# A hybrid diffusion backbone on one core: the RWKV-7 units without GpSimd instructions

## The chip, the core and the metric

The program runs on one core of one Trainium2 chip. The metric is the device time of one execution in microseconds (us); lower is better. The engines are named as in the profile: PE (matrix products, with its weight loads as PEld), DVE (vector), ACT (scalar), POOL (GpSimd) and SP, whose queue issues the DMAs spoken of here.

## What is computed

Layer 0 is attention and is not touched. Layer 1 runs two branches on 1024 latent and 256 context tokens, and the change is in its RWKV-7 branch: 8 heads of 64 features, scanned in both directions, first over the context and then over the latents.

```python
kk = k * k_k;  kk = kk * rsqrt(sum(kk * kk, per head) + 1e-12)
for d in (forward, backward):
    decay = exp(-exp(w_log[d]))                  # w_log: a gate of every token and feature
    a = sigmoid(a0[d] + da @ a_up[d])
    k_d = k * (1 + (a - 1) * k_a);   b = kk * a
    s = s * decay - (s @ kk) b^T + v k_d^T       # per token, s is 64 x 64
    y = s @ r
out = groupnorm(y_fwd + y_bwd) + sum(r * (k_fwd + k_bwd)/2 * r_k) * v
x = x + gate * ([out * silu(g), hyena] @ w_out);   rms_norm(x)
```

## The kernel before, in words

All products that need accuracy are made from float32 values split in two parts, "hi" and "lo": `split` copies the hi part on ACT (L164) and subtracts it for the lo part (L168) on POOL, or on DVE where `lo_eng="v"`.

**Projections** (`gemm3`, to about 1796 us). Blocks of 128 columns of the input projection follow each other: values, keys (`rw_keys`, four blocks, one for each pair of heads j), then four blocks of r. Each block is 48 or 72 products g_ps at L363 out of `mm3`, and needs its weights split on DVE (w_lo, L168). `rw_gates` runs beside them: the decay gates so go token by token to the DRAM tensor SG (L1266), the rates a to AS (L1275). `rw_keys` makes kk with a reciprocal on DVE (L1219) and stores kk and k in KK (L1223). An r block ends with one DVE instruction rwo (L1028) and a store to US.

**Units** (`rwkv`). There are 8 jobs (j, d) of 5 units, 40 units in all, each of 256 tokens (4 chunks of 64) for two heads. The loop over units b issues `rw_solve` for b+2, `rw_front` for b+12, `rw_trans` and `rw_scan` for b; a list scheduler then sets the final order on each engine from its own estimates, and each engine works through its list in order.

- `rw_front` loads kk and k (kkf, L1381), a (af), the gates (sg, L1386) and v, splits the gates (ACT, then POOL), forms running sums cs_ps on PE (L1397), then exponentials on ACT (E and AKR). POOL makes `kd` in two steps (L1417, L1419), `af` (L1420) and half of BK (L1426); DVE the other half (L1424) and AK, AR (L1415, L1414). PE forms the Gram matrices g_ps (L1442), four products for head 0 and then four for head 1, with 64 rows each. DVE masks one half of g_ps to la (L1443); the other half goes through an ACT copy (L1446) and a POOL mask (L1447) into gm. ACT copies the off-diagonal blocks of la into LO (L1452), a tile whose other entries are zero. la's diagonal blocks go by DMA to lanes (LD, L1458).
- `rw_invert` inverts these blocks of 32 tokens for a job at once: L1495 and L1497 on DVE, 31 steps of two instructions each, from L (loaded from LD) to XD. The first job does it in two parts (units 0 to 1, then 2 to 4), the others in one.
- `rw_solve` (L1522) is y = XT R, z = LO Z, R = R - z on DVE (L1529), w = XT R: three groups of four products of 128 rows and 128 columns, all in one PSUM bank "s".
- `rw_trans` makes the transitions ph_ps (L1555). `rw_scan` carries the state over the four chunks: st_ps (L1579, L1582), one ACT copy S (L1583), and two ACT copies into a block-diagonal tile (L1590) for the output product L1591; L1593 adds gm times UV after each chunk.
- `rw_bonus` and `rw_readout` serve the 16 backward latent units; five POOL instructions on [128, 4] (L1640 to L1647) are the group norm's root, L1614 to L1617 the bonus, L1656 the gate.

Every float32 product stands twice in the profile, as two MATMUL records; the scheduler's listing below has it once. So g_ps with 8 products a unit has 16 records.

**Final** (`Final`, from unit 28 on) prepares the output projection in the room that the units leave: `weights` loads rec_w_out in 16 pieces, multiplies by the gate (POOL, L1943) and splits it; `project` makes fe_ps (L363).

The PSUM tiles of a front take turns in two banks "f"; "s" and "p" hold one tile at a time:

```python
FB = 2
PB = (1, 1, 1, 1, 1)                          # banks s, p, t, y, r
tags = [...  for t in ("sfff" if self.nfront < 5 else "rfty" if self.nfront < 10 else "ffff")]
ps = self.rps([128, 4, 128], "g_ps", *tags[1])          # in rw_front, once for each head
ps = self.rps([128, 2, 512], "ph_ps", "p", PB[1])       # in rw_trans
```

## Time and profile before

| | |
|---|---|
| median of 3 runs | 2480.67 us (2476.8 to 2485.05) |
| profiled execution, first to last instruction | 2478.4 us |
| PE busy | 2300.1 us (93%), 16639 products |
| DVE busy | 1543.9 us (62%), 3275 instructions |
| ACT busy | 1191.4 us (48%), 2815 instructions |
| POOL busy | 981.2 us (40%), 1071 instructions |
| DMA | 357.09 MB, 144 GB/s on average |

The profiled execution has no time of its own beside its span; the span lies 2.3 us under the median of the runs. The page's slices and the table of stretches tell which engine is full where; the groups by line tell what one instruction of a kind takes and which wait ended before it; the timeline tells what ran beside what.

### The profile page before, as it was taken

Reading aid. Unit: us, or ns where it says so; the run is one execution under the profiler, and the core shown is the slowest. Engines: PE = TensorE matmul, PEld = TensorE weight load, DVE = VectorE, ACT = ScalarE, POOL = GpSimd, SP = SyncE. Lnnn points to the kernel's source line nnn. Section 1 sums busy time; section 2 is a strip of 40 time slices with the busy share of each in tenths; the row PEclk is TensorE's granted clock in tenths of the full one; section 3 lists DMA queues with packets and bytes.
Section 4 is the critical chain, followed back from the end, with each engine's and each line's share of the span. In section 5 each row is a group of like instructions: output and inputs, shape, how many; then the busy total and the mean of one; then the engine's idle time right before and its main releaser. Section 6 shows DMA issues by size and latency. Waiting matters only on the chain. (4 is left out here: it accounts for less than half of the span.)

```text
span 2478.4 us, 45316 instructions
## 1 busy us (share of the span) xinstructions
PE 2300.1 (93%) x16639; PEld 1883.1 (76%) x16639; DVE 1543.9 (62%) x3275; ACT 1191.4 (48%) x2815; POOL 981.2 (40%) x1071
## 2 busy tenths in 40 slices
PE   5999999999999998888899999899977999999997
...
GB/s 280 129 128 115 127 157 145 221 165 38 112 82 77 158 174 188 177 185 178 156 133 135 124 225 138 147 215 184 158 111 111 121 113 131 114 130 132 170 81 95
DMA packets 337269, 357.09 MB, mean 144 GB/s; under 512 B 80082, under 2 KB 274911, under 8 KB 336278
## 3 DMA queue, kind: packets, MB, share of 16 engines
...
q0 software_dynamic: 144, 4.19, 0.4%
...
## 5 line engine op out<-in xcount | busy, mean ns | idle before, releaser
L363 PE MATMUL g_ps<-xl,w_hi 128*128 128x512 f32 x1056 | 269.3, 401 | 1.0 <-ACT w_hi L164 1.0
L363 PEld LDWEIGHTS g_ps<-xl,w_hi 128*128 128x128 f32 x1056 | 200.2, 192 | 44.3 <-issue 1.9
L413 POOL TENSOR_TENSOR al_acc<-al_acc,al_t 128x512 f32<-128x512 f32 x98 | 130.0, 1327 | 182.7 <-ACT al_t L411 153.0
L168 DVE TENSOR_TENSOR w_lo<-w_raw,w_hi 128x256 fp32r<-128x256 f32 (+1 forms) x184 | 126.8, 745 | 78.6 <-PE g_ps L363 40.3
L159 ACT COPY pt<-pt_ps 128x512 f32<-128x512 f32 (+1 forms) x235 | 105.9, 459 | 138.1 <-PE pt_ps L641 136.3
L630 PE MATMUL s_ps<-k,q 128*128 128x256 f32 (+1 forms) x352 | 140.3, 405 | 18.6 <-DMA k<-ka 11.2
L1497 DVE TENSOR_TENSOR X<-X,tmp 80x112 f32<-80x112 f32 (+25 forms) x279 | 139.0, 498 | 6.7 <-DVE tmp L1495 0.2
L1495 DVE TENSOR_TENSOR tmp<-L,X 80x112 f32<-80x112 f32 (+25 forms) x279 | 130.5, 468 | 13.2 <-DMA L<-LD 7.0
L363 PE MATMUL g_ps<-xl,w_lo 128*128 128x512 f32 x528 | 138.3, 396 | 0.0
L363 PE MATMUL g_ps<-xhi,w_hi 128*128 128x512 f32 (+1 forms) x528 | 119.0, 368 | 9.3 <-DVE ac_res L255 4.7
L631 PE MATMUL s_ps<-k,q 128*128 128x256 f32 (+1 forms) x352 | 118.0, 341 | 4.9 <-DMA k<-ka 4.9
L411 ACT ACTIVATE al_t<-al_w,condT 128x512 f32<-128x512 f32 x98 | 70.8, 722 | 102.8 <-POOL al_acc L413 63.7
L658 ACT ACTIVATE p<-p,mn 128x1280 f32<-128x1280 f32 (+1 forms) x96 | 103.4, 1077 | 31.9 <-DVE p L655 30.1
L363 PE MATMUL g_ps<-xhi,w_lo 128*128 128x512 f32 (+1 forms) x528 | 118.3, 363 | 0.0
L363 PEld LDWEIGHTS g_ps<-xl,w_lo 128*128 128x128 f32 x528 | 98.6, 189 | 21.2 <-issue 1.4
L363 PEld LDWEIGHTS g_ps<-xhi,w_hi 128*128 128x128 f32 x528 | 90.4, 194 | 31.0 <-DVE qraw L521 6.1
L363 PE MATMUL g_ps<-xlo,w_hi 128*128 128x512 f32 (+1 forms) x528 | 112.8, 356 | 0.0
L641 PE MATMUL pt_ps<-ident,p 128*128 128x128 f32 x704 | 110.8, 280 | 1.5 <-ACT pt L159 0.6
L168 POOL TENSOR_TENSOR hz<-hfull,hz 128x256 fp32r<-128x256 f32 x64 | 47.4, 742 | 152.9 <-ACT hz L164 152.2
L669 PE MATMUL o_ps<-pt,vb 128*64 128x128 f32 x1344 | 104.6, 279 | 0.0
L363 PEld LDWEIGHTS g_ps<-xhi,w_lo 128*128 128x128 f32 x528 | 89.6, 191 | 18.1 <-issue 5.0
L800 POOL TENSOR_TENSOR bias<-namask,tt 128x384 f32<-128x384 f32 x64 | 64.8, 1021 | 97.3 <-DMA tt<-TG 39.6
...
## 6 DMA issues: line engine op xcount, KB each, us to landing
...
```

The source lines that it names most:

```text
L159: self.nc.scalar.copy(out=out, in_=in_)
L168: e.tensor_tensor(out=lo, in0=full, in1=hi.bitcast(F32), op=ALU.subtract)
L363: nc.tensor.matmul(ps, x(k), y(k), start=(n == 0), stop=(n == 3 * nk - 1))
L411: nc.scalar.activation(out=o, in_=wt, func=AF.Copy, scale=self.condT[:, k, ci:ci + 1])
L413: nc.gpsimd.tensor_tensor(out=t, in0=t, in1=o, op=ALU.add)
L630: self.nc.tensor.matmul(ps, q, k[0][ks], start=True, stop=False)
L631: self.nc.tensor.matmul(ps, q, k[1][ks], start=False, stop=True)
L641: nc.tensor.transpose(ps[:, c, :], p[:, (c4 + c) * 128:(c4 + c + 1) * 128], self.ident)
L658: nc.scalar.activation(out=p[:, 0:nk], in_=p[:, 0:nk], func=AF.Exp, bias=mn, scale=-1.0, accum_out=rs[:, hh:hh + 1])
L669: nc.tensor.matmul(o[64 * hh:64 * hh + 64, :], v[c][hh], pts[hh][:, c, :], start=(c == 0), stop=(c == nch - 1), tile_position=(0, 64 * hh))
L1495: nc.vector.tensor_tensor(out=tv, in0=L[:, s:s + 1, rt].to_broadcast([n, nj, nt]), in1=X[:, rj, s:s + 1].to_broadcast([n, nj, nt]), op=ALU ...
L1497: nc.vector.tensor_tensor(out=X[:, rj, rt], in0=X[:, rj, rt], in1=tv, op=ALU.subtract)
```

## The change

All that POOL did for the units moves or goes. (1) `rw_keys` forms b = kk a and k_d for both directions beside the projections and stores kk, b and k_d in KB (one for each direction); `rw_gates` splits the gates there and stores both parts. A front then loads both ready. (2) Both masks are applied on DVE straight from PSUM, into one tile LG that holds gm (columns 0 to 63) and la (64 to 127). (3) The Gram products alternate between the heads, in two banks. (4) LO is gone: the solve multiplies 32 x 32 blocks of LG, and the correction is added to w_ps in PSUM by a second product instead of a subtraction on DVE. (5) The state is written by two ACT copies straight into the block-diagonal tile, and the four products of gm with UV stand together ahead of the chunks. (6) Bonus, readout and the final weights use DVE.

The diff, cut to its core:

```diff
@@ rw_keys
-        for i, t in enumerate((kk, o)):
-            nc.sync.dma_start(out=self.KK[rows, :, i, :], in_=t.rearrange("p (q t) -> p q t", t=256))
+        for d in range(2):
+            b = sp.tile([128, NT], F32, name="kb", tag="lraw", bufs=2)
+            nc.sync.dma_start(out=b, in_=self.AS[d][rows, :])
+            kd = sp.tile([128, NT], F32, name="kd", tag="kd", bufs=1)
+            nc.scalar.activation(out=kd, in_=b, func=AF.Identity, scale=self.col("rwkv_k_a", j), bias=self.oka[:, j:j + 1])
+            nc.vector.tensor_tensor(out=kd, in0=kd, in1=o, op=ALU.mult)
+            nc.vector.tensor_tensor(out=b, in0=b, in1=kk, op=ALU.mult)
+            for i, t in enumerate((kk, b, kd)):
+                nc.sync.dma_start(out=self.KB[d][rows, :, i, :], in_=t.rearrange("p (q t) -> p q t", t=256))
@@ rw_gates
-                nc.sync.dma_start(out=self.SG[d][tt * 128:tt * 128 + 128, :], in_=so)
+                sh = sp.tile([128, 2, 512], F32R, name="sh", tag="sh", bufs=2)
+                self.split(sh[:, 0], sh[:, 1], so, lo_eng="v")
+                for part in range(2):
+                    nc.sync.dma_start(out=self.SG[d][tt // 2, :, :, part, tt % 2, :], ...)
@@ rw_front
-... ("sfff" if self.nfront < 5 else "rfty" if self.nfront < 10 else "ffff")]
+... ("sffff" if self.nfront < 5 else "rffty" if self.nfront < 10 else "fffff")]
-        self.split(sgs[:, 0], sgs[:, 1], sg)
-            nc.vector.tensor_tensor(out=AR, in0=AR, in1=v3(rf), op=ALU.mult)
-        nc.vector.tensor_tensor(out=AK, in0=AK, in1=kv, op=ALU.mult)
-        nc.gpsimd.tensor_scalar(out=kd, in0=v3(af), scalar1=self.col("rwkv_k_a", j), ...)
-        nc.gpsimd.tensor_tensor(out=kd, in0=kd, in1=kf, op=ALU.mult)
-        nc.gpsimd.tensor_tensor(out=v3(af), in0=v3(af), in1=kv, op=ALU.mult)
+            nc.vector.tensor_tensor(out=AKR, in0=AKR, in1=kb[:, 0:2].rearrange(...), op=ALU.mult)
-        self.last_bk = nc.gpsimd.tensor_tensor(out=BK[:, :, 64:192], in0=kd, in1=E, op=ALU.mult)
+        nc.vector.tensor_tensor(out=BK[:, :, 64:192], in0=v3(kb[:, 3]), in1=E, op=ALU.mult)
+        gp = [self.rps([128, 4, 128], "g_ps", *tags[1 + h]) for h in range(2)]
+        for ci in range(4):
+            for h in range(2):
+                z = slice(64 * h, 64 * h + 64)
+                nc.tensor.matmul(gp[h][:, ci, c0:128], BK[z, i, 128 * c:128 * c + 128], ...)
         for h in range(2):
-            nc.vector.tensor_tensor(out=la[:, h], in0=ps[:, :, 0:64], in1=mask[:, 0:64]..., op=ALU.mult)
-                nc.scalar.copy(out=gm[:, h], in_=ps[:, :, 64:128])
-                nc.gpsimd.tensor_tensor(out=gm[:, h], in0=gm[:, h], in1=mask[:, 64:128]..., op=ALU.mult)
-            for c in range(2):
-                nc.scalar.copy(out=LO[zs, 2 * h:2 * h + 2, t1:t1 + 32], in_=la[zs, h, c::2, t0:t0 + 32])
+            nc.vector.tensor_tensor(out=LG[:, h, :, c0:128], in0=gp[h][:, :, c0:128], in1=mask[:, c0:128]..., op=ALU.mult)
@@ rw_solve
-        ps = prod(xt, R, "y_ps")
+        ps = self.rps([128, 4, 128], "w_ps", "s", PB[0])
+        for u in range(4):
+            nc.tensor.matmul(ps[:, u, :], xt[:, u, :], R[:, u, :], start=(u == 0), stop=True, skip_group_check=True)
         nc.scalar.copy(out=Z, in_=ps)
-        ps = prod(LO, Z, "z_ps")
-        nc.vector.tensor_tensor(out=R, in0=R, in1=ps, op=ALU.subtract)
-        ps = prod(xt, R, "w_ps")
+        pz = self.rps([128, 2, 512], "z_ps", "p", PB[1])...
+        for u in range(4):
+            for c in range(2):
+                nc.tensor.matmul(pz[zt, u, :], LG[zs, h, 2 * i + c, 64 + t0:96 + t0], Z[zs, u, :], ...,
+                                 tile_position=(64 * c + s0, 64 * c + t0))
+        for c in range(2):
+            nc.scalar.activation(out=Z[zt], in_=pz[zt], func=AF.Copy, scale=-1.0)
+        for u in range(4):
+            for c in range(2):
+                nc.tensor.matmul(ps[zt, u, :], xt[zt, u, zt], Z[zt, u, :], start=False, stop=True, ...,
+                                 tile_position=(64 * c + t0, 64 * c + t0))
@@ rw_scan
+        if lat:
+            for i in range(2):
+                for h, zo in heads:
+                    for c in range(2):
+                        nc.tensor.matmul(yp[64 * c:64 * c + 64, i, zo], LG[:, h, 2 * i + c, 0:64], UV[:, i, c, h, :],
+                                         start=(i == 0 and h == 0), stop=False, tile_position=(0, 64 * c))
-            nc.scalar.activation(out=n, in_=ps, func=AF.Copy, scale=Dt[:, n0 + ci:n0 + ci + 1])
+            for h, zo in heads:
+                nc.scalar.activation(out=n[zo, zo], in_=ps[zo], func=AF.Copy, scale=Dt[zo, n0 + ci:n0 + ci + 1])
-                    nc.scalar.copy(out=sd[zo, zo], in_=S[zo])
-                    nc.tensor.matmul(yp[zc, i, zo], gm[:, h, ci, :], UV[:, i, c, h, :], ...)
@@ rw_bonus, rw_readout, Final.weights
-        nc.gpsimd.tensor_tensor(out=a0, in0=a0, in1=a1, op=ALU.add)
+        nc.vector.tensor_tensor(out=a0, in0=a0, in1=a1, op=ALU.add)
-        e = nc.gpsimd
+        e = nc.vector
-        nc.gpsimd.tensor_tensor(out=t, in0=t, in1=g, op=ALU.mult)
+        nc.vector.tensor_tensor(out=t, in0=t, in1=g, op=ALU.mult)
-            self.nc.gpsimd.tensor_tensor(out=raw, in0=raw, in1=self.gate1[h], op=ALU.mult)
-            self.k.split(tiles[0][h], tiles[1][h], raw)
+            self.nc.vector.tensor_tensor(out=raw, in0=raw, in1=self.gate1[h], op=ALU.mult)
+            self.k.split(tiles[0][h], tiles[1][h], raw, lo_eng="v")
```

The scheduler's listing shows where this moves work. On PE, at the end of the projections, before the change (g_ps<-xl is the projection, cs_ps the first step of a front, g_ps<-AKR its Gram products):

```order
L363 MATMUL g_ps<-xl_12457,w_lo 128x512 x8
L363 MATMUL g_ps<-xl_12457,w_hi 128x512 x3
L1397 MATMUL cs_ps<-tri,sgs 128x256
L363 MATMUL g_ps<-xl_12457,w_hi 128x512 x5
L363 MATMUL g_ps<-xl_12458,w_hi 128x512
L1397 MATMUL cs_ps<-tri,sgs 128x256 x3
L363 MATMUL g_ps<-xl_12458,w_hi 128x512 x7
L363 MATMUL g_ps<-xl_12457,w_lo 128x512 x8
L363 MATMUL g_ps<-xl_12457,w_hi 128x512 x8
L1397 MATMUL cs_ps<-tri,sgs 128x256 x4
L363 MATMUL g_ps<-xl_12458,w_hi 128x512 x4
L1442 MATMUL g_ps<-AKR,BK 128x64 x8
```

And now:

```order
L363 MATMUL g_ps<-xl_12458,w_hi 128x512 x8
L363 MATMUL g_ps<-xl_12459,w_hi 128x512 x8
L363 MATMUL g_ps<-xl_12458,w_lo 128x512 x8
L1402 MATMUL cs_ps<-tri,sgs 128x256 x8
L1436 MATMUL g_ps<-AKR,BK 128x64 x8
L1402 MATMUL cs_ps<-tri,sgs 128x256 x4
L1450 MATMUL bk_ps<-ident,BK 128x128 x4
L1457 MATMUL rh_ps<-ident,AKR 128x2x64 x2
```

The first steps of the fronts stood among the last two blocks of the projection; they now follow its last product.

On PE in the middle of the units, before (y_ps and z_ps are the solve, yo_ps<-UV,gm the second output product):

```order
L1522 MATMUL y_ps<-R,XT_18018 128x128 x4
L1579 MATMUL st_ps<-UV,BT 64x64 x2
L1582 MATMUL st_ps<-S,PH 64x64 x2
L1397 MATMUL cs_ps<-tri,sgs 128x256
L1591 MATMUL yo_ps<-S_18035,RT 64x128
L1593 MATMUL yo_ps<-UV,gm 64x64 x2
L1397 MATMUL cs_ps<-tri,sgs 128x256 x3
L1555 MATMUL ph_ps<-BT,At 64x64 x2
L1522 MATMUL z_ps<-Z,LO_17313 128x128 x4
L1579 MATMUL st_ps<-UV,BT 64x64 x2
L1582 MATMUL st_ps<-S,PH 64x64 x2
```

And now:

```order
L1577 MATMUL yo_ps<-UV,LG 64x64 x8
L1586 MATMUL st_ps<-UV,BT 64x64 x2
L1589 MATMUL st_ps<-S_18070,PH 64x64 x2
L1595 MATMUL yo_ps<-S_18070,RT 64x128
L1402 MATMUL cs_ps<-tri,sgs 128x256 x3
L1520 MATMUL z_ps<-Z,LG 32x128 x8
L1586 MATMUL st_ps<-UV,BT 64x64 x2
L1589 MATMUL st_ps<-S_18071,PH 64x64 x2
L1595 MATMUL yo_ps<-S_18071,RT 64x128
L1648 MATMUL yt_ps<-ident,Y 128x128 x2
L1528 MATMUL w_ps<-Z,XT_18060 32x128 x8
L1554 MATMUL ph_ps<-BT,At 64x64 x8
```

The output products stand in one group of eight, and the solve's second and third group have eight products of 32 x 128 in place of four of 128 x 128.

On DVE, at the last key block, before (RECIPROCAL is L1219, w_lo the weights of the next projection block, LO the zeroed tiles):

```order
L1219 RECIPROCAL ksq<-ksq 128x256
L168 TENSOR_TENSOR w_lo<-w_raw,w_hi 128x256 x4
L1219 RECIPROCAL ksq<-ksq 128x512
L1028 SCALAR_TENSOR_TENSOR rwo<-rws,hm,rwo 128x1024
L1219 RECIPROCAL ksq<-ksq 128x512
L168 TENSOR_TENSOR w_lo<-w_raw,w_hi 128x256 x4
L1169 MEMSET LO_17312 128x512
```

And now:

```order
L1216 RECIPROCAL ksq<-ksq 128x256
L1216 RECIPROCAL ksq<-ksq 128x512
L1225 TENSOR_TENSOR kd<-kd,rwo 128x1280
L1226 TENSOR_TENSOR kb<-kb,kk 128x1280
L168 TENSOR_TENSOR w_lo<-w_raw,w_hi 128x256 x4
L1028 SCALAR_TENSOR_TENSOR rwo<-rws,hm,rwo 128x1024
L1216 RECIPROCAL ksq<-ksq 128x512
L1225 TENSOR_TENSOR kd<-kd,rwo 128x1280
L1226 TENSOR_TENSOR kb<-kb,kk 128x1280
L1028 SCALAR_TENSOR_TENSOR rwo<-rws,hm,rwo 128x1024
L1225 TENSOR_TENSOR kd<-kd,rwo 128x1280
L1226 TENSOR_TENSOR kb<-kb,kk 128x1280
```

Between the reciprocals stand the products kd and kb of 1280 columns, the last of them behind the weights of the last projection block and behind the third rwo.

## Rows read from the trace of the kernel before

**Rows 1.** Busy us by stretch: PE, PEld, DVE, ACT, POOL, clock, DMA, GB/s

```profile
1640.00:1700.00 60.00, 58.51 (x314) 49.76 (x313) 33.19 (x51) 38.97 (x76) 13.29 (x10) 1.00 0.81 273
1700.00:1783.00 83.00, 83.00 (x381) 66.79 (x380) 62.07 (x54) 47.16 (x82) 40.13 (x41) 1.00 0.42 137
...
1810.00:1885.00 75.00, 53.50 (x360) 44.63 (x360) 70.80 (x156) 29.70 (x92) 40.52 (x51) 0.59 0.36 98
1885.00:2265.00 380.00, 368.09 (x4245) 305.16 (x4245) 294.46 (x690) 252.20 (x835) 227.27 (x322) 0.99 0.45 121
2265.00:2310.00 45.00, 37.22 (x382) 29.95 (x381) 42.44 (x75) 23.70 (x71) 32.15 (x37) 0.92 0.54 163
```

**Rows 2.** PE groups from 1885 to 2265 us: count | busy us, mean ns

```profile
L1442 PE MATMUL g_ps<-AKR,BK 64*128 64x128 f32 (+1 forms) x464 | 57.1, 291 | 2.8 <-DVE AKR L1414 1.1 <-POOL BK L1426 1.0 <-POOL Dt L1407 0.3
...
L1473 PE MATMUL rh_ps<-V,la 64*64 64x64 f32 x464 | 20.1, 224 | 0.0
```

**Rows 3.** Timeline from 2020 us, PE: start, length, line, operation, count

```profile
2021.44 1.16 PE L1522 MATMUL z_ps<-Z,LO 128*128 128x128 f32 x8
...
2022.53 0.93 PE L1442 MATMUL g_ps<-AKR,BK 64*128 64x128 f32 x6
...
2024.19 0.39 PE L1593 MATMUL yo_ps<-UV,gm 128*64 128x64 f32 x4
...
2026.41 0.34 PE L1579 MATMUL st_ps<-UV,BT 128*64 128x64 f32 x4
```

**Rows 4.** Chain of waits, 1740 to 1960 us: start, length, what

```profile
1896.96 0.61 PE rh_ps L1473 x16
```

**Rows 5.** Chain of waits, 1960 us to the end

```profile
2068.91 2.91 DMA LD<-la
2071.87 3.54 DMA L<-LD
...
2243.12 1.64 PE g_ps L1442 x16
```

**Rows 6.** Timeline from 2025 us, DVE beside POOL

```profile
2025.38 0.41 DVE L1495 TENSOR_TENSOR tmp<-L,X 80x252 f32<-80x252 f32 x1
...
2025.94 0.77 POOL L1447 TENSOR_TENSOR gm<-gm 128x256 f32<-128x256 f32 x1 [0.80 <-ACT gm L1446]
2026.04 0.94 DVE L1497 TENSOR_TENSOR X<-X,tmp 80x252 f32<-80x252 f32 x1
```

**Rows 7.** DVE groups by shape, 1800 to 2310 us

```profile
L1443 DVE TENSOR_TENSOR la<-g_ps,gm 128x256 f32<-128x256 f32 x78 | 32.1, 414 | 13.0 <-PE g_ps L1442 12.4
L1529 DVE TENSOR_TENSOR R<-R,z_ps 128x512 f32<-128x512 f32 x34 | 23.0, 677 | 4.3 <-PE z_ps L1522 4.3
L1415 DVE TENSOR_TENSOR AKR<-AKR,kkf 128x256 f32<-128x256 f32 x37 | 21.5, 580 | 0.1
```

**Rows 8.** POOL groups, 1600 us to the end

```profile
L1426 POOL TENSOR_TENSOR BK<-kd,E 128x256 f32<-128x256 f32 x40 | 38.8, 971 | 67.8 <-ACT E L1399 46.5 <-issue 8.4 <-DMA LD<-la 7.8
...
L1614 POOL TENSOR_TENSOR ioa<-ioa,iob 128x256 f32<-128x256 f32 x16 | 12.6, 786 | 23.6 <-DMA iob<-AS 19.0 <-issue 4.6
...
L1943 POOL TENSOR_TENSOR fgm<-fgm,fAKR 128x512 f32<-128x512 f32 x8 | 10.7, 1337 | 16.5 <-DMA fgm<-rec_w_out 15.6 <-DMA fAKR<-AD 0.9
...
L1644 POOL TENSOR_TENSOR gvr<-gvr,grs 128x4 f32<-128x4 f32 x16 | 3.7, 233 | 13.5 <-ACT grs L1643 13.5
```

**Rows 9.** Single lines: count, ns min/median/max, first and last start us

```profile
L1397 PE MATMUL cs_ps<-tri,sgs x160: 276/282/580, 1783.2 to 2252.0; 128*128 128x256 f32 x160
...
L363 PE MATMUL g_ps<-xl,w_lo x528: 387/389/803, 1233.9 to 1796.4; 128*128 128x512 f32 x176
...
L1495 DVE TENSOR_TENSOR tmp<-L,X x279: 176/396/1457, 1810.5 to 2319.2; 80x31 f32<-80x31 f32 x8, 80x87 f32<-80x87 f32 x8, 80x135 f32<-80x135 f32 x8, 80x175 f32<-80x175 f32 x8
```

**Rows 10.** ACT groups, 1600 us to the end

```profile
L1583 ACT ACTIVATE S<-st_ps,Dt 128x64 f32<-128x64 f32 x160 | 50.4, 315 | 83.3 <-PE st_ps L1582 81.1 <-PE st_ps L1579 0.7
...
L1527 ACT COPY Z<-y_ps 128x512 f32<-128x512 f32 x40 | 23.5, 587 | 19.3 <-PE y_ps L1522 18.7
```

More of the change, by code (lines that the diff above doesn't have):

```diff
@@ L1160, in rw_init @@
         C = self.C = {}
-        tri = fp.tile([128, 2, 256], F32, name="tri0", tag="kkf", bufs=2)
+        tri = fp.tile([128, 2, 256], F32, name="tri0", tag="BK", bufs=2)
         nc.sync.dma_start(out=tri, in_=a["k_tri"].rearrange("d p k -> p d k"))
@@ L1166, in rw_init @@
         nc.sync.dma_start(out=C["gm"], in_=a["k_gmask"].rearrange("d p k -> p d k"))
-        C["LO"] = [[self.ep.tile([128, 4, 128], F32, name=f"LO0{i}", tag="LO0", bufs=5) for i in range(5)]]
-        for t in C["LO"][0]:
-            nc.vector.memset(t, 0.0)
-        o = self.vofs["rwkv_k_a"]
-        C["oka"] = fp.tile([128, 4], F32, name="oka", bufs=1)
-        nc.vector.tensor_scalar(out=C["oka"], in0=self.vec[:, o:o + 4], scalar1=-1.0, scalar2=1.0, op0=ALU.mult, op1=ALU.add)
     def rw_table(self):
@@ L1204, in rw_pre @@
         nc.vector.memset(self.e12, 1e-12)
+        o = self.vofs["rwkv_k_a"]
+        self.oka = sp.tile([128, 4], F32, name="oka")
+        nc.vector.tensor_scalar(out=self.oka, in0=self.vec[:, o:o + 4], scalar1=-1.0, scalar2=1.0, op0=ALU.mult, op1=ALU.add)
     def rw_keys(self, j, o, sp, pp):
@@ L1293, in rwkv @@
                 nc.sync.dma_start(out=C[n], in_=a["k_" + n])
-            C["LO"].append([kp.tile([128, 4, 128], F32, name=f"LO1{i}") for i in range(5)])
             C["S"] = [kp.tile([128, 128], F32, name=f"S{i}") for i in range(4)]
@@ L1415, in rw_front @@
-        nc.vector.tensor_tensor(out=AK, in0=AK, in1=kv, op=ALU.mult)
-        kd = fp.tile([128, 2, 128], F32, name="kd", bufs=1)
-        nc.gpsimd.tensor_scalar(out=kd, in0=v3(af), scalar1=self.col("rwkv_k_a", j), scalar2=C["oka"][:, j:j + 1],
-                                op0=ALU.mult, op1=ALU.add)
-        nc.gpsimd.tensor_tensor(out=kd, in0=kd, in1=kf, op=ALU.mult)
-        nc.gpsimd.tensor_tensor(out=v3(af), in0=v3(af), in1=kv, op=ALU.mult)
+            nc.sync.dma_start(out=kb[:, 0], in_=self.US[rows, tok])
@@ new lines, in rw_front @@
+        nc.vector.tensor_tensor(out=BK[:, :, 64:192], in0=v3(kb[:, 3]), in1=E, op=ALU.mult)
+        LG = wp.tile([128, 2, 4, 128], F32, name="LG", bufs=bufs)
+        mask = C["gm"][:, d, :]
+        c0 = 0 if lat else 64
+        gp = [self.rps([128, 4, 128], "g_ps", *tags[1 + h]) for h in range(2)]
+        for ci in range(4):
+            i, c = divmod(ci, 2)
+            zc = slice(64 * c, 64 * c + 64)
+            for h in range(2):
+                z = slice(64 * h, 64 * h + 64)
+                nc.tensor.matmul(gp[h][:, ci, c0:128], BK[z, i, 128 * c:128 * c + 128],
+                                 AKR[z, i, :, zc] if lat else AK[z, i, zc], start=True, stop=True)
@@ L1935, in take, with pair @@
                          bufs=1 if tag in "LX" else 5 if pool is self.k.ep else 7)
+    def pair(self, pool, dt=F32R):
+        t = self.take(pool, "LG", dt, (128, 2, 512))
+        return [t[:, i] for i in range(2)]
     def weights(self, k, tiles):
@@ L2003, in after @@
         if b == 28:
-            self.raws = [take(wp, "gm", F32) for _ in range(2)]
+            self.raws = self.pair(wp, F32)
             self.gate1 = [take(ep, t, F32) for t in ("AKR", "BT")]
@@ L2007, in after @@
                 nc.sync.dma_start(out=self.gate1[h], in_=k.AD[1][0, 2 * D + 512 * h:2 * D + 512 * h + 512].partition_broadcast(128))
-            self.fm = [take(ep, t) for t in ("R", "gm")]
+            self.fm = self.pair(ep)
             for n in range(4, 8):
@@ L2016, in after @@
             lx = [take(ep, t, F32R, (128, D)) for t in "LX"]
-            self.weights(0, four(lambda i, h: take(ep, "LO0")))
+            self.weights(0, [self.pair(wp) for _ in range(2)])
             self.weights(1, [[t[:, z] for z in self.cs] for t in lx])
         if b == 34:
-            self.weights(2, four(lambda i, h: take(wp, "gm")))
-            self.weights(3, [[take(wp, "gm"), take(wp, "R")], [take(wp, "R"), take(ep, "LO0")]])
+            self.weights(2, [self.pair(wp) for _ in range(2)])
+            self.weights(3, [self.pair(wp), [take(wp, "R") for _ in range(2)]])
         if b == 36:
@@ L2027, in after @@
                 k.m3[q] = take(ep, t, F32R, (128, 2, 256))
-            self.fn = [take(ep, t, F32) for t in ("R", "gm")]
+            self.fn = self.pair(ep, F32)
             for h in range(2):
```

116 lines of the change are left out of this document (45 added, 71 removed).

## Prediction

> **What bounds the kernel now.** I read the table of stretches first [rows 1], because the change touches only the time from about 1640 us on and the limits differ there. Until 1783 us PE is full (83.00 of 83 us): projection products. From 1810 to 1885 us PE is idle for a third and runs at a granted clock of 0.59, while DVE is busy for 70.80 of 75 us: the first job's inverses have to be made before any solve can start. From 1885 to 2265 us PE is again busy for 368 of 380 us at clock 0.99, DVE for 294 and POOL for 227. From 2265 to 2310 us DVE is full (42.44 of 45). Then the output projection holds PE.
>
> The groups by line give the middle stretch its unit: 464 records of g_ps, 16 to a unit, so 29 units in 380 us, 13.1 us each [rows 2]. The chain of waits and the timeline then show what one group of products takes [rows 3 to 5]: 16 records of g_ps 1.64 us; 8 of the solve 1.16; 4 of yo_ps 0.39; 4 of st_ps 0.34; 16 of rh_ps, whose products lie in alternating quarters of the array, only 0.61. That last row is the key to the PE part.
>
> DVE beside POOL: an inverse step of 252 columns takes 0.41 us alone and 0.94 us while POOL masks gm [rows 6]. By shape, AKR of 256 columns, with both inputs in SBUF, averages 580 ns, while la, of the same size but reading PSUM, stays at 414 [rows 7]. So POOL's instructions cost DVE time, and masks read from PSUM escape that.
>
> **The change, part by part.**
>
> *Gram products.* Before, eight records for one head follow each other on the same 64 rows; now the heads alternate, on different rows and into different banks. A record of 128 columns costs 1.64/16 = 0.10 us now [rows 5]. rh_ps, alternating, costs (0.61-0.22)/15 = 0.026 us for 64 columns, 0.05 for 128 [rows 4], the 0.22 being one record's own length [rows 2]. A group would be 0.05 x 15 + 0.29 = 1.0 us: 0.6 to 0.7 saved in a unit. If rows alone do not run beside each other, nothing is saved.
>
> *Output products.* yo_ps<-UV takes 0.39 us for four records in a row, st_ps, which alternates between column halves, 0.34 [rows 3]. Sixteen of them in one alternating group save four times 0.05 and some starts: 0.3 us a unit, between 0.1 and 0.5.
>
> *Solve.* First group as before. Second and third: 16 records of 32 rows instead of 8 of 128. Alternating in pairs, 15 x 0.05 + 0.27 = 1.0 to 1.2 us against 1.16 now [rows 3]: nothing gained or lost. No row shows products of 32 rows; if they ran one behind another, a group would be 16 x 0.10 + 0.2 = 1.8, 0.7 more. The subtraction of 0.68 us on DVE [rows 7] becomes two ACT copies of up to 0.59 each [rows 10]; the chain of a solve is about 0.5 longer, but it has 13 us, so I count nothing. PE does other units' work meanwhile.
>
> *Sum on PE:* 0.65 + 0.3 is about 1.0 us a unit, x 29 = 29 us in the middle stretch, and 3 us later.
>
> *DVE and ACT in the units.* DVE gains half of BK (0.41), wider masks (2 x 0.26), loses R (0.68) and one start: +0.2 us a unit; readout and bonus bring 2 us for each of 16 backward units. That is about 28 us over the stretch. The slowing by POOL, 0.17 us on every instruction like AKR [rows 7] and up to 0.5 on a long inverse step, is worth about as much or more over 690 instructions. So DVE stays near 290 us, cover enough at 73 to 83% of the stretch. ACT loses the gm and LO copies; the state is now two copies in a row instead of one of 315 ns [rows 10], 0.2 to 0.3 us on a chain that waits for PE anyway. Waits on POOL in a front (BK waited 67.8 us for E and others in all, [rows 8]) go; late next is DVE. I add 4 us for that: middle stretch -33.
>
> *Projections.* DVE gets 16 products of 1280 columns. From 0.41 for 256 and 0.68 for 512 [rows 7] I extrapolate 1.46 us each, an estimate: 23 us beside 62 of 83 busy [rows 1]. It is then full there, and the scheduler places some ahead of the last w_lo. The DMAs: 8 stores of 640 KB (128 x 1280 float32, by the code) become 24 stores and 8 loads, 15.7 MB more, at the 273 GB/s seen at share 0.81 [rows 1] 58 us against 48 us of free share until 1783. Twenty gate tiles are stored twice: 5 MB, 19 us against 11 free before 1700. All this covers itself only if PE's weights come first; the listing has the last weight load ahead of half of the key stores. On SP's queue these are 24 more issues, in order, and 20 more for the gates; a front then issues one load fewer (kb and one tile of gates for kkf, af, rf and sg) and a bonus one fewer, so the queue gets shorter where the units wait for it. I take +3 us, from 0 to +17 (the transfers' overhang).
>
> *Start of the units.* The first cs_ps began at 1783.2 us, the last projection product at 1796.4, the first inverse step at 1810.5 [rows 9]. Now cs_ps follows the last product. From there two fronts without POOL hops (about 6 us from the rows above), the store of la (2.91) and the load of L (3.54, [rows 5]) give 1796.4 + 3 + 12.5 = 1812: +2 us. Then, by the listing, DVE has between the first inverse step and the end of the first job 21 masks at 0.68 instead of 16 at 0.41, 18 halves of BK instead of 8, 7 wide AKR (0.68) instead of 10, and 11 bonus steps: +17 us; without POOL some 10 us go: the 34 front instructions are 14 us at 0.41 and the 124 steps 47 at 0.38, an estimate just under their median of 0.396 [rows 9], against 70.80 [rows 1]. +7 us, part of which is work done early. Start: +9, from -5 to +20.
>
> *Final weights.* 32 instructions of 0.68 us move to DVE, from 2255 to 2320 us, where it is full; POOL's 32 us of interference go. I count 0, from -10 to +21.
>
> *End:* POOL steps of the last readout become shorter, -1; with the 3 us above -4.
>
> **Sum:** +3 + 9 - 33 - 4 = -25 us. The profiled span of 2478.4 us becomes 2453; the median of the runs lies 2.3 us above that span, so 2456.
>
> **What speaks against it.** In the timeline the solve's 8 records start at 2021.44 and the next group, of another row count, 1.09 us later [rows 3], while 8 records at 0.10 are 0.8: a change of shape seems to cost 0.2 to 0.3 us. Groups of 32 rows are a new shape between all others: up to four more changes in a unit. At 0.2 us each that is 0.8 us x 39 units = 31 us. The Trainium skill, TensorEngine Tiling (Array Packing), Key Properties, says that changing the tiling mode, not just the tile, drains the engine; as far as this one row goes the trace agrees, and by that rule the time would be that of the second price of rival A.
>
> **The rivals.**
>
> *A, slower: products of 32 rows do not overlap.* Place: second and third group of every solve. Price: 0.7 x 2 x 29 = 41 us in the middle stretch and 14 in the ten units beside the output projection, where PE is also full: 2456 + 55 = 2511. With 0.2 us for each change of shape instead, 31 us: 2487. It decides once the two groups take 0.5 us each more than now, which eats the whole 1.0. For: no such product is in the trace, and the solve's group above ends late. Against: rh_ps with 64 rows overlaps fully, sharing one bank. Chance 0.15 (0.05 for 2511, 0.10 for the drain).
>
> *B, no change: DVE's waits take the place of POOL's.* DVE works in order, and now stands itself where POOL waited: 23.6 us for bonus loads, 13.5 for ACT inside the readout, and 21 for final weights, half of it in the row shown [rows 8]. Behind it stand masks and inverse steps. If half of these 58 us reach the end, the time is 2456 + 25 = 2481. Against: between 1885 and 2265 us DVE has 85 us free. Chance 0.13.
>
> *C, slower start.* The key stores' overhang of 17 us and DVE's backlog delay the first fronts fully: 2456 + 20 = 2476. Chance 0.10.
>
> *D, faster: the units are bound by waits, not by products.* 4245 records in 380 us are 90 ns each, though many alternate at 26; if in-order waits for POOL and slowed DVE cost PE 1.2 us a unit beyond my 1.0, the time is 2456 - 35 = 2421. For: waits on POOL's instructions and on la are spread over every front. Chance 0.16.
>
> **How the numbers follow.** The forecast itself, 2440 to 2472, has 0.46. About 0.3%, 7 us, is what a measurement of this kernel can tell. Faster by more: forecast 0.46, D 0.16, and a third of C and B: 0.70. Within 7 us: the rest of C and of B, 0.13. Slower: A, and the tails of C: 0.17. Range 2412 to 2492: it leaves out the worst of A and the far end of D.
>
> **What would show it.** In the profile after: g_ps x16 near 1.0 us; yo_ps<-UV x16 near 0.6; z_ps and the second w_ps group at 1.0 to 1.2 each (1.8 is A); inverse steps of 252 columns at 0.41 throughout; the units' stretch near 12 us a unit; first inverse step near 1815 us, end of the first job near 1895. I am wrong if the middle stretch stays at 13 us a unit, or if PE is idle in the projections.

## Result: slower, 2572.85 us, ratio 1.037

The changed kernel takes 2572.85 us (median of 4 runs, 2566.36 to 2583.92), the kernel before 2480.33 (2476.8 to 2485.05). The ratio is 1.037, with a 95% interval of 1.0336 to 1.0405. The prediction was 2456, with a range to 2492: wrong in sign and outside the range. The profiled execution spans 2564.6 us, 86.2 more than that of before.

Two lines of its page, the busy time of each engine and, in 40 slices of the span, the granted clock in tenths of the full one; under them the clock line of before:

```profile
PE 2341.0 (91%) x17279; PEld 1874.3 (73%) x17279; DVE 1533.5 (60%) x3433; ACT 1182.3 (46%) x2565; POOL 650.0 (25%) x595
...
PEclk7999999999999898989999999999666878869999
```

```profile
PEclk7999999999999999999999999999967999999999
```

POOL has 331 us less to do than before, and PE 41 more. Before, the clock fell in two slices late in the program, ahead of the first solves; now it is low in eight in a row, through most of the units. (The first slice is the program's beginning in both; the three 8s near 1000 us lie in code that the change doesn't touch.)

The stretches of the changed kernel, columns as in [rows 1], its two last rows inside the units:

```profile
1640.00:1700.00 60.00, 55.59 (x285) 45.15 (x286) 40.23 (x60) 39.88 (x77) 13.79 (x9) 1.00 0.94 288
1700.00:1783.00 83.00, 77.00 (x355) 60.89 (x354) 71.78 (x60) 56.92 (x95) 44.62 (x28) 1.00 0.82 262
...
1806.60:1847.60 41.00, 19.48 (x124) 16.69 (x123) 16.94 (x32) 11.04 (x30) 4.88 (x6) 0.65 0.86 266
1847.60:1922.90 75.30, 55.44 (x408) 44.61 (x406) 62.53 (x168) 18.66 (x48) 0.00 (x0) 0.64 0.48 138
...
2280.00:2300.00 20.00, 20.00 (x169) 14.22 (x170) 17.76 (x52) 8.39 (x23) 0.00 (x0) 0.50 0.31 88
2120.00:2140.00 20.00, 20.00 (x302) 15.79 (x300) 10.92 (x33) 12.37 (x36) 0.00 (x0) 1.00 0.50 135
```

The last two rows are the case in small. PE is busy for all of 20 us in both; with the clock at 1.00 (the upper level, 2.4 GHz) 302 records start, at 0.50 (1.2 GHz) 169.

I cut both executions at three events: the last projection product, the first z_ps and the last z_ps. The stretch from the first to the last z_ps, of before and then of the changed kernel:

```profile
1883.60:2412.50 528.90, 508.67 (x5447) 416.17 (x5446) 370.20 (x833) 308.15 (x1005) 287.20 (x390) 0.98 0.45 125
```

```profile
1922.90:2494.70 571.80, 535.72 (x5988) 400.38 (x5988) 322.75 (x918) 292.38 (x786) 7.71 (x14) 0.84 0.40 112
```

The last projection product starts at 1796.4 us before and at 1806.6 now (+10). From there to the first z_ps it is 87.2 us before and 116.3 now (+29). First to last z_ps grows by 43, the tail from 65.9 to 69.9 (+4). The clock has two levels, so a mean of 0.84 is 2 x 0.16 = 0.32 of the stretch at the lower one: 183 us, against 21 before at 0.98. I use that conversion throughout; with a clock of two digits it is good to some 5 us (the clock's own records in the two traces add up to 179 and 17).

Products of the units in the changed kernel's timeline (start, length, line, count), the first four at the upper level, the last at the lower:

```profile
2041.66 1.06 PE L1520 MATMUL z_ps<-Z,LG 32*32 32x128 f32 x16
2042.65 0.70 PE L1617 MATMUL bo_ps<-ioa,ones 128*128 128x256 f32 x2
...
2104.57 1.16 PE L1436 MATMUL g_ps<-AKR,BK 64*128 64x128 f32 x16
...
2139.76 0.64 PE L1577 MATMUL yo_ps<-UV,LG 128*64 128x64 f32 x16
...
2271.65 0.33 PE L1589 MATMUL st_ps<-S,PH 64*64 64x64 f32 x4 [2.25 <-DVE PH L1557]
...
2272.78 1.88 PE L1520 MATMUL z_ps<-Z,LG 32*32 32x128 f32 x16
```

At the upper level every group takes about what the prediction gave it: z_ps 1.06, with the next group 0.99 behind its first record; g_ps 1.16 (1.64 in [rows 5]); yo_ps 0.64. Ahead of the fall at 2272.9 us PE had stood 2.25 us for DVE's PH; behind it the 16 records of z_ps take 1.88, and the clock stays down until 2310.4 us, though PE is busy for 35.6 of these 37.5 us. The stretch at the lower level from 1938.4 us is fuller still, 33.97 of 34.1 us:

```profile
1938.40:1972.50 34.10, 33.97 (x303) 25.46 (x304) 23.42 (x64) 15.87 (x42) 0.00 (x0) 0.50 0.18 51
```

DVE, by shape, from 1900 to 2250 us; mean ns of one is the figure behind the busy time:

```profile
L1423 DVE TENSOR_TENSOR BK<-kb,E 128x256 f32<-128x256 f32 x23 | 9.7, 422 | 14.9 <-ACT E L1404 14.6
...
L1484 DVE TENSOR_TENSOR tmp<-L,X 80x252 f32<-80x252 f32 x10 | 4.2, 416 | 0.2
```

The inverse steps of 252 columns take 416 ns throughout, where one beside POOL's mask lasted 0.94 us in [rows 6].

DVE's products of 1280 columns in the projections, beside POOL, which kept rws and kk there:

```profile
1763.91 1.49 DVE L1225 TENSOR_TENSOR kd<-kd,rwo 128x1280 f32<-128x1280 f32 x1
1764.42 2.73 POOL L1026 TENSOR_TENSOR rws<-ul 128x1024 f32<-128x1024 f32 x1 [4.26 <-ACT ul L1008]
1765.32 3.18 DVE L1226 TENSOR_TENSOR kb<-kb,kk 128x1280 f32<-128x1280 f32 x1
```

Of the 16, the seven that began while POOL had no rws or kk in hand took 1.42 to 1.49 us. The nine that began beside one took 1.90 to 3.18: the rest of POOL's instruction and about 1.35 us more (here 1.83 + 1.35).

### The profile page after: what moved, and what is told of

It is laid out like the page before. It is cut to its first block, busy times and chain, and to the rows that moved or that the text cites. A ratio compares the mean times of both kernels' runs of the same rounds, so it can differ in the third digit from the quotient of the medians.

```text
span 2564.6 us, 45745 instructions
## 1 busy us (share of the span) xinstructions
PE 2341.0 (91%) x17279; PEld 1874.3 (73%) x17279; DVE 1533.5 (60%) x3433; ACT 1182.3 (46%) x2565; POOL 650.0 (25%) x595
## 5 line engine op out<-in xcount | busy, mean ns | idle before, releaser
L168 DVE TENSOR_TENSOR w_lo<-w_raw,w_hi 128x256 fp32r<-128x256 f32 (+1 forms) x184 | 121.4, 716 | 60.8 <-ACT w_hi L164 31.8
L1592 ACT ACTIVATE S<-st_ps,Dt 64x64 f32<-64x64 f32 x320 | 98.6, 308 | 97.9 <-PE st_ps L1589 91.9
L1478 POOL MEMSET X<- 80x1024 f32 (+2 forms) x9 | 8.5, 947 | 481.6 <-DMA XD<-X 303.6
L1484 DVE TENSOR_TENSOR tmp<-L,X 80x112 f32<-80x112 f32 (+28 forms) x279 | 93.7, 336 | 23.5 <-DMA L<-LD 12.7
L363 PEld LDWEIGHTS g_ps<-xlo,w_hi 128*128 128x128 f32 x528 | 89.6, 191 | 15.0 <-issue 1.1
```

Source lines behind the costliest of these rows:

```text
L168: e.tensor_tensor(out=lo, in0=full, in1=hi.bitcast(F32), op=ALU.subtract)
L363: nc.tensor.matmul(ps, x(k), y(k), start=(n == 0), stop=(n == 3 * nk - 1))
L1484: nc.vector.tensor_tensor(out=tv, in0=L[:, s:s + 1, rt].to_broadcast([n, nj, nt]), in1=X[:, rj, s:s + 1].to_broadcast([n, nj, nt]), op=ALU ...
L1592: nc.scalar.activation(out=n[zo, zo], in_=ps[zo], func=AF.Copy, scale=Dt[zo, n0 + ci:n0 + ci + 1])
```

## The experiments

All times are medians; ratios are to the kernel before on the same chip. The clock and the lengths are those of the profiled execution of each.

| run | ratio (95%) | last projection product to first z_ps, us | first to last z_ps, us | clock there |
|---|---|---|---|---|
| before | 1 | 87.2 | 528.9 | 0.98 |
| changed | 1.037 (1.0336 to 1.0405) | 116.3 | 571.8 | 0.84 |
| E1 old solve | 0.9958 (0.9933 to 0.9983) | 116.5 | 480.9 | 0.99 |
| E2 new solve alone | 1.0432 (1.0391 to 1.0473) | 84.3 | 620.7 | 0.84 |
| E3 four idle products more | 1.0282 (1.0219 to 1.0344) | 116.7 | 560.4 | 0.94 |
| E4 Gram serial | 1.0449 (1.0385 to 1.0513) | 119.3 | 606.1 | 0.82 |
| E5 keys in fronts | 1.0012 (0.9994 to 1.0029) | 96.2 | 518.0 | 0.94 |
| E6 gates in fronts | 1.0029 (1.0009 to 1.005) | 130.7 | 491.6 | 0.97 |
| E7 two kd tiles | 1.0015 (0.9998 to 1.0032) | 102.1 | 516.9 | 0.95 |
| E8 second group large | 1.0174 (1.014 to 1.0207) | 119.3 | 535.1 | 0.91 |
| E9 regrouping alone | 0.999 (0.9972 to 1.0007) | 89.3 | 531.4 | 0.95 |
| E10 POOL in fronts | 0.9867 (0.9838 to 0.9896) | 94.6 | 493.9 | 0.98 |
| E11 E10 without regrouping | 0.9986 (0.9968 to 1.0003) | 96.2 | 526.8 | 0.95 |
| E12 E10 without POOL | 0.9972 (0.9956 to 0.9989) | 102.0 | 508.9 | 0.96 |

### E1, the old solve in the changed kernel

```diff
-                nc.tensor.matmul(pz[zt, u, :], LG[zs, h, 2 * i + c, 64 + t0:96 + t0], Z[zs, u, :], start=(u == 0), stop=(u == 3),
...
-            nc.scalar.activation(out=Z[zt], in_=pz[zt], func=AF.Copy, scale=-1.0)
...
-                nc.tensor.matmul(ps[zt, u, :], xt[zt, u, zt], Z[zt, u, :], start=False, stop=True, skip_group_check=True,
...
+                nc.scalar.copy(out=LO[zs, 2 * h:2 * h + 2, t1:t1 + 32], in_=la[zs, h, c::2, t0:t0 + 32])
...
+        ps = prod(LO, Z, "z_ps")
+        nc.vector.tensor_tensor(out=R, in0=R, in1=ps, op=ALU.subtract)
+        ps = prod(xt, R, "w_ps")
```

> The changed kernel with the solve of before: one copied tile of off-diagonal blocks, three groups of four 128-row products, the subtraction on DVE; all else as changed. Theory 1 (the clock: groups of 32-row, 32-column products let the granted clock fall, 0.84 between the first and the last z_ps against 0.98 before): with 128-row products back the clock there returns to 0.95 or more, the stretch of 571.7 us shrinks to 515 to 540, the time to 2515 to 2540 us; the 39 us lost ahead of the first z_ps stay. Theory 2 (units wait for DVE and for chains; the clock falls because PE stands idle): the stretch stays within 560 to 580 and the time within 2560 to 2585, since PE gets as much work as before and four ACT copies more.

Measured 2475.59 us. First to last z_ps:

```profile
1918.90:2399.80 480.90, 458.92 (x5398) 363.57 (x5396) 338.67 (x963) 284.41 (x866) 11.38 (x21) 0.99 0.48 133
```

The clock is back at 0.99 and the stretch is 90.9 us shorter than in the changed kernel, more than theory 1 asked for, and so is the time below its range. With 183 us at the lower level against 10, half of the difference is 87 us: the clock pays for nearly all of it. Theory 2 is out. The profiled execution (2467.9 us) is the fastest of ten runs, 8 us under their median, so up to 8 us of its gain are luck.

### E2, the new solve alone

```diff
+        la = wp.tile([128, 2, 4, 64], F32, name="la", bufs=bufs)
-        ps = prod(LO, Z, "z_ps")
-        nc.vector.tensor_tensor(out=R, in0=R, in1=ps, op=ALU.subtract)
-        ps = prod(xt, R, "w_ps")
+                nc.tensor.matmul(pz[zt, u, :], la[zs, h, 2 * i + c, t0:32 + t0], Z[zs, u, :], start=(u == 0), stop=(u == 3),
...
+                nc.tensor.matmul(ps[zt, u, :], xt[zt, u, zt], Z[zt, u, :], start=False, stop=True, skip_group_check=True,
```

> The kernel before with the new solve alone (32-row products out of la, the sum in PSUM; la kept until the solve, the copies of off-diagonal blocks left out). Theory 1 (clock): the granted clock between the first and the last z_ps falls from 0.98 to 0.90 or less and the time rises to 2500 to 2560 us, although no product got slower at full clock. Theory 2 (waits): clock 0.96 or more, time 2465 to 2490.

Measured 2590.97 us, above theory 1's range.

```profile
1884.30:2505.00 620.70, 569.28 (x6033) 449.53 (x6034) 337.34 (x792) 325.03 (x958) 271.11 (x383) 0.84 0.38 104
```

91.8 us more between first and last z_ps than before, and half of 199 - 21 us at the lower level is 89. Taken out of one kernel or put into the other, the new solve costs the same.

### E3, products that nobody reads

```diff
+        for u in range(4):
+            nc.tensor.matmul(pf[:, u % 4, :], xt[:, u % 4, :], R[:, u % 4, :], start=True, stop=True)
```

> The changed kernel with four more 128-row, 128-column products in every solve, whose sums nobody reads, behind z_ps: work added, nothing taken away. Theory 1 (clock): clock between first and last z_ps 0.90 or more, and the time falls by 10 to 50 us, to 2520 to 2560, although PE has 0.9 us more to do in each of 40 units at full clock. Theory 2 (waits): the products either fill idle time of PE (same time, within 2565 to 2580) or add up to 35 us (2580 to 2610).

Measured 2553.96 us: with more work the kernel is 19 us faster than the changed one, as only theory 1 allows. That is 0.9%, and the intervals of the two ratios just touch (1.0219 to 1.0344 and 1.0336 to 1.0405); the clock, 0.94 against 0.84, is the clearer sign.

```profile
1927.40:2487.80 560.40, 531.66 (x6308) 409.50 (x6308) 322.89 (x922) 291.97 (x786) 7.71 (x14) 0.94 0.42 114
```

At the lower level it spends 67 us instead of 183, worth 58; the eight added records cost 40 x 8 x 0.11 = 35, an estimate. The stretch gained 11 of the 23 that remain.

### E4, the Gram products head by head

```diff
-        for ci in range(4):
-            for h in range(2):
+        for h in range(2):
+            for ci in range(4):
```

> The changed kernel with the Gram products of a unit head by head again, as before, in their two banks. Theory 1 (clock by the solve's small products): 16 records cost 0.6 us more at full clock, the clock stays 0.82 to 0.88: 2570 to 2600 us. A rival, theory 3 (it is the overlap of the alternating Gram products that empties PE's time and lets the clock fall): clock 0.92 or more and 2510 to 2550.

Measured 2598.21 us; the clock stays low (0.82). Theory 3 is out. At the upper level a unit's 16 Gram records take 1.71 us here, against the 1.16 shown above, so the interleave saves the 0.6 us that was said:

```profile
2060.39 1.71 PE L1436 MATMUL g_ps<-AKR,BK 64*128 64x128 f32 x16
```

What it is worth in time is rough. The stretch is 34 us longer, of which 17 are half of 218 - 183 us at the lower level, and the rest about 0.6 us for each of the 28 units whose Gram products lie there; but this profiled execution is the slowest of its four and that of the changed kernel the fastest. The medians are 25 us apart, and the intervals of the ratios overlap.

### E8, one of the two groups made large

```diff
+        if n % 5 == 0:
+            nc.gpsimd.memset(Z2, 0.0)
-            nc.scalar.activation(out=Z[zt], in_=pz[zt], func=AF.Copy, scale=-1.0)
+            nc.scalar.activation(out=Z2[zt], in_=pz[zt], func=AF.Copy, scale=-1.0)
-                nc.tensor.matmul(ps[zt, u, :], xt[zt, u, zt], Z[zt, u, :], start=False, stop=True, skip_group_check=True,
+            nc.tensor.matmul(ps[:, u, :], xt[:, u, :], Z2[:, u, :], start=False, stop=True, skip_group_check=True)
```

> The changed kernel with one of the two groups of small products made large: the correction goes into a tile whose other rows are zero and w_ps adds four products of 128 rows and 128 columns instead of eight of 32; z_ps stays at 32 rows. At full clock either group takes about 1.0 to 1.1 us. Theory 1 (clock by small products): half of the cause, so time at half clock between first and last z_ps between the 9 us of E1 and the 179 of the changed kernel, 20 to 120; stretch 495 to 545 us, time 2485 to 2545. A rival (the sum in PSUM or the order of the solve costs the time, whatever the size): stretch 560 to 580, time 2560 to 2585.

Measured 2529.47 us.

```profile
1926.40:2461.50 535.10, 497.71 (x5676) 386.28 (x5676) 319.17 (x917) 293.54 (x785) 11.44 (x21) 0.91 0.43 119
```

With one small group instead of two the time at the lower level is 96 us, between 10 and 183, and the stretch lies between those of E1 and of the changed kernel. The sum in PSUM is still there, so it isn't the cause; the size of the products is. Which part of the size does it (rows, columns, or 16 records in place of 8) no run separates.

Could it be PE's waits instead? E12 below decides that. There PE stands idle for 39.8 of 508.9 us, in the changed kernel for 36.1 of 571.8, and the clock is 0.96 against 0.84:

```profile
1895.10:2404.00 508.90, 469.12 (x5368) 371.37 (x5368) 367.44 (x1048) 310.09 (x928) 11.29 (x21) 0.96 0.45 122
```

Waits do start the falls. Between first and last z_ps the clock falls 11 times in the changed kernel and 7 times in E9, and each of these 18 falls follows a wait of PE, as at 2272.9 us. What differs most is how long the clock then stays down: 15 us on average with both groups small (18 in E2), 9 in E8, 10 in E3, 7 in E9, where no group is small. PE is busy for 170 of the changed kernel's 179 us at the lower level.

### E5 to E7, the start of the units

E5 puts the key products back into the fronts, E6 the splitting of the gates, E7 gives kd a second tile; each is an edit of E1.

```diff
-            for i, t in enumerate((kk, b, kd)):
-                nc.sync.dma_start(out=self.KB[d][rows, :, i, :], in_=t.rearrange("p (q t) -> p q t", t=256))
+        for i, t in enumerate((kk, o)):
+            nc.sync.dma_start(out=self.KK[rows, :, i, :], in_=t.rearrange("p (q t) -> p q t", t=256))
...
+        nc.scalar.activation(out=kd, in_=kb[:, 2], func=AF.Identity, scale=self.col("rwkv_k_a", j), bias=C["oka"][:, j:j + 1])
+        nc.vector.tensor_tensor(out=kb[:, 3], in0=kb[:, 3], in1=kd, op=ALU.mult)
+        nc.vector.tensor_tensor(out=kb[:, 2], in0=kb[:, 2], in1=kb[:, 1], op=ALU.mult)
```

```diff
-                self.split(sh[:, 0], sh[:, 1], so, lo_eng="v")
...
+        self.split(sgs[:, 0], sgs[:, 1], sg, lo_eng="v")
```

```diff
-            kd = sp.tile([128, NT], F32, name="kd", tag="kd", bufs=1)
+            kd = sp.tile([128, NT], F32, name="kd", tag="kd", bufs=2)
```

> E1 (old solve) with the key products back in the fronts: kk and k stored once a block, b and k_d formed for each unit, two products on DVE and one scaling on ACT; nothing on POOL. In E1 the first z_ps starts 116.5 us behind the last projection product, in the kernel before 87.1. Theory K (the first loads of the fronts stand in SP's queue behind the last key stores, which wait for products on DVE that wait for one kd tile): the first cs_ps starts within 5 us of the last projection product instead of 15 behind it, that distance falls to 85 to 100 us, and the time to 0.980 to 0.990 of the kernel before (2440 to 2462), although DVE has 0.8 us more in each unit. Theory D (DVE's masks and halves of BK hold the start): the distance stays 110 to 120, the time 0.993 to 1.002.

> E1 with the gates stored once and split in the fronts (ACT and DVE), key products as changed. Theory K: the last projection product comes 2 to 6 us earlier (less DMA traffic before 1700 us), the distance to the first z_ps stays 110 to 120; time 0.990 to 0.998 of the kernel before. Rival, theory G (the doubled gate stores hold the start): the distance falls to 100 or less and the time to 0.988 or less.

> E1 with two kd tiles instead of one, nothing else. Theory K: the wait of ACT's kd for the store of the last one goes, the last key store and with it the first loads of the fronts leave 5 to 15 us earlier; distance 100 to 112 us, time 0.990 to 0.995 of the kernel before. Theory D: no change, 0.993 to 0.999.

The chain of waits of the changed kernel shows what held its start (start, length, what):

```profile
1765.43 7.52 DMA KB<-kd
1773.03 1.47 ACT kd L1224
...
1776.32 7.87 DMA KB<-kd
...
1801.79 4.96 DMA KB<-kd
1806.82 1.46 ACT kd L1224
...
1809.71 3.19 DVE kb L1226
1813.53 0.59 SPq L1302
...
1816.81 5.18 DMA sgs<-SG
1822.13 1.21 PE cs_ps L1402 x4
```

Each kd waits for the store of the one before it; the last key product ends at 1812.9, and only behind the issue of its store can SP issue the loads of constants (L1302) and of the first front. So the first cs_ps comes 15.5 us behind the last projection product (1806.6) instead of 13 ahead of it.

On the start theory K holds for E5: it brings the first cs_ps to 1791.7, 11.6 us ahead of the last projection product, and the distance from 116.5 to 96.2. E7 takes 14 us off the distance, but only in part as theory K has it: ACT's kd no longer waits for the store (22.3 us in E1, none in E7), yet the first cs_ps still comes 9.8 us behind the last projection product (14.7 in E1), and the chain to it now runs through the last projection products. So the one kd tile is a part of the delay. E6 brings the last projection product from 1802.4 to 1796.7, as it should, but lengthens the distance by 14, which neither of its theories allows. The times all miss their expectation: 2487.33, 2489.3 and 2486.3 us, none faster than E1. What the start gave in E5 and E7 (20 and 14 us), the stretch of the units took back with 37 and 36, at a clock of 0.94 and 0.95.

Why is open. E7 differs from E1 in one number, but the scheduler's list for PE differs from that place on, through all units, and y_ps waited there 10.5 us for the inverses' DMA where it waited 2.9 in E1. Every variant here has an order of its own, so differences below some 1% mix an edit with the order that it drew.

### E9 to E12, which part of the units' gain is whose

E9 is the kernel before with the Gram products alternating and the output products in one group. E10 is E1 with key products and gates in the fronts and on POOL. E11 takes the regrouping out of E10; E12 moves E10's front work from POOL to DVE and ACT.

E9:

```diff
-        for h in range(2):
-            z = slice(64 * h, 64 * h + 64)
-            ps = self.rps([128, 4, 128], "g_ps", *tags[1])
-            for ci in range(4):
+        gp = [self.rps([128, 4, 128], "g_ps", *tags[1 + h]) for h in range(2)]
+        for ci in range(4):
...
+            for h in range(2):
...
+                        nc.tensor.matmul(yp[64 * c:64 * c + 64, i, zo], gm[:, h, 2 * i + c, :], UV[:, i, c, h, :],
```

E10, beside the edits of E5 and E6 (E12 is these with DVE and ACT in the places of POOL):

```diff
+        nc.gpsimd.tensor_scalar(out=kd, in0=kb[:, 2], scalar1=self.col("rwkv_k_a", j), scalar2=C["oka"][:, j:j + 1],
...
+        nc.gpsimd.tensor_tensor(out=kb[:, 3], in0=kb[:, 3], in1=kd, op=ALU.mult)
+        nc.gpsimd.tensor_tensor(out=kb[:, 2], in0=kb[:, 2], in1=kb[:, 1], op=ALU.mult)
...
+        self.split(sgs[:, 0], sgs[:, 1], sg)
```

E11, against E10:

```diff
-        for ci in range(4):
...
-            for h in range(2):
+        for h in range(2):
...
+            for ci in range(4):
...
+                    nc.tensor.matmul(yp[zc, i, zo], LG[:, h, ci, 0:64], UV[:, i, c, h, :], start=False, stop=(h == 1),
```

> The kernel before with two parts of the change alone: the Gram products of the heads alternate in two banks, and the products of the masked Gram halves with UV stand together ahead of the chunks. Solve, masks, key products, gates and POOL's work as before. Prediction's prices: 0.65 + 0.3 us of PE for each of 29 units, 28 us less: 0.985 to 0.991 of the kernel before (2447 to 2462 us), clock between first and last z_ps still 0.97 or more. Rival, theory 4 (with less PE work in a unit PE stands idle more, waits for DVE and POOL, and the clock falls now and then): more than 40 us at half clock between first and last z_ps, time 0.993 to 1.003.

> E1 with key products and gate parts back in the fronts and on POOL (three products and the lo part of the gates), masks from PSUM, half of BK, readout and final weights on DVE as changed. Start as in the kernel before: last projection product at 1794 to 1799 us, first z_ps 85 to 95 us behind it, since nothing of the keys' and gates' stores is added. Theory 4 (units at the edge of the clock): between first and last z_ps 485 to 520 us with 10 to 60 us at half clock, time 0.982 to 1.000 of the kernel before. If POOL's interference with DVE is what the units suffer from (the rival of the prediction's DVE term): 515 us or more and 1.000 to 1.010.

> E10 with the Gram products head by head again and the products of the masked Gram with UV back in the loop over chunks: masks from PSUM and the rest of E10 stay. E9 showed the regrouping alone to be worth nothing. If it is worth nothing here either (theory M: the gain of E10 is that of the masks, with POOL's mask and ACT's copy out of the fronts), 0.984 to 0.990 of the kernel before (2443 to 2458 us). If products and masks need each other (theory P: in E9 PE's saved time went into waits for POOL and slowed DVE, in E10 it counts), 28 us come back: 0.995 to 1.001.

> E10 with the work of the fronts that is on POOL there put on DVE and ACT in the fronts: two products and the lo part of the gates on DVE (3 x 0.41 us a unit), one scaling on ACT. If POOL's slowing of DVE weighs more than its help (the prediction's view), 0.980 to 0.987 of the kernel before; if DVE's added 1.2 us a unit delay PE and let the clock fall (theory 4), 0.993 to 1.005, with 30 us or more at half clock between first and last z_ps.

E9 measured 2478.49 us. Two PE groups of it from 1896 to 2250 us (busy, mean | idle before and its releasers):

```profile
L1442 PE MATMUL g_ps<-AKR,BK 64*128 64x128 f32 (+1 forms) x422 | 34.8, 286 | 7.5 <-DVE AKR L1414 3.4 <-POOL BK L1426 3.3 <-DVE AKR L1415 0.6
...
L1463 PE MATMUL bk_ps<-ident,BK 128*128 128x128 f32 x104 | 18.4, 304 | 9.2 <-ACT gm L1448 8.7 <-DVE la L1445 0.4
```

The products did get faster: g_ps is busy for 34.8 us in 422 records, against 57.1 in 464 before [rows 2]. But bk_ps now waits 9.2 us, nearly all for ACT's copy gm on its way to POOL's mask, g_ps 7.5 for DVE and POOL, and the clock fell to 0.95, 53 us at the lower level instead of 21. Nothing measurable is left of 28 us, which is the outcome of theory 4.

E10 measured 2449.74 us: faster than both kernels, than the one before by 1.0 to 1.6%. The same two groups of it:

```profile
L1438 PE MATMUL g_ps<-AKR,BK 64*128 64x128 f32 (+1 forms) x448 | 36.6, 292 | 0.6 <-DVE AKR L1414 0.5
...
L1452 PE MATMUL bk_ps<-ident,BK 128*128 128x128 f32 x112 | 19.0, 294 | 1.3 <-DVE LG L1441 1.2
```

With the masks read from PSUM neither group waits (0.6 and 1.3 us), and the saved time counts: 35 us between first and last z_ps. E11, with the masks but without the regrouping, falls back to 2480.47 us. So theory P: each half alone is worth nothing that can be measured, both together 1.3%. (E10 and E11 keep the smaller parts of the change too; that it is the masks that count is read from the waits, not tested apart.) E12, without POOL, measured 2478.08 us at a clock of 0.96. That is theory 4's outcome: 0.9972, with 41 us at the lower level. POOL does slow DVE in E10, where the inverse steps of 252 columns average 476 and 552 ns against 416 and 413 in the changed kernel, but its help is worth more. The caveat on orders holds for these runs too, which are 1% apart; the products' times and the waits shown don't depend on it.

## Why the prediction was wrong, point by point

- **Gram and output products**: right. 1.16 us against 1.0 predicted, and 0.64 against 0.6.
- **Solve, "nothing gained or lost"**: the step that failed. Its duration was right (1.06 us, within 1.0 to 1.2), its effect was not: it cost 91 us, nearly all through the granted clock. I costed a group of products by its length at the clock of before and never asked whether the clock would stay. Both levels were in the rows, 0.99 in the units and 0.59 in the starved stretch [rows 1], and I took the low one for a matter of idle time alone. Waits start the falls, but the row at 2280 us shows that they don't hold the clock down: PE busy for 20.00 of 20 us, clock 0.50. With the two groups of 128-row products back (E1) or taken out (E2) the clock between first and last z_ps is 0.99 and 0.84, with one of them back 0.91 (E8), with four unread ones added 0.94 (E3).
- The Trainium skill, TensorE: Matmul & The Clock Gate, Part 1, lets the clock follow how busy the engine has been. The falls behind waits agree with that. Taken as the profile counts busy time, the length of the low stretches does not: 20.00 of 20 us at 0.50, and 20.00 of 20 at 1.00.
- **Rival A** named the right place (second and third group of every solve) and the right side, with the wrong mechanism and a price too small (31 to 55 us). At the upper level the 32-row products overlap: 16 records, and the next group 0.99 us behind the first. The Trainium skill, TensorEngine Tiling (Array Packing), Key Properties, has a change of tiling mode drain the engine; those 0.99 us contain whatever that costs, and they are less than the 1.09 us from the old group's first record to the next group [rows 3].
- **Rivals B and D** did not come. B (2481; half of its 58 us would be 29, not 25) had DVE's waits eat the gain, but in E1, with DVE's work as changed, the stretch got 48 us shorter. D's 2421 was reached by no version; the fastest is E10 with 2449.74.
- **Sum on PE, -33**: E1's stretch is 48 us shorter than before, so the size was near, but the reason was not PE alone. E9 shows the regrouping worth nothing while masks pass through ACT and POOL; E11 shows the masks, with the other parts of E10, worth nothing alone. "PE busy for 368 of 380 us" hid that the next wait lay close behind.
- **DVE**: right in kind. Inverse steps at 416 ns, DVE busy for 338.7 of 480.9 us in E1, 70%.
- **Projections, +3**: +10 measured, inside 0 to +17. From the first to the last product of xl it is 569 us before, 578 now, 572 in E6 and 574 in E5, so about 6 us of it are the doubled gate stores and 4 the key products. DVE's products of 1280 columns averaged 1.87 (kd) and 2.52 us (kb). The 1.46 was right for one by itself (1.42 to 1.49); what I left out is POOL, whose slowing of DVE I had counted in the units and not here.
- **Start, +9**: mis-sized, +29. The transfers were counted as bytes; the chain shows order. One kd tile chained the stores, and SP's queue held the first loads behind the last of them. E5, which takes away bytes and order both, gives back 20 of the 29. In E10 to E12, where keys and gates are stored as before, the distance is still 94.6 to 102.0 us against 87.2, so 7 us or more have another cause, which is open. This is rival C's place, at more than its price.
- **Final weights and end, 0 and -4**: the tail grew by 4; with the old solve in E1 it is 65.9 us again, as before.
